# Sums of the modulation on VectorE in a two-layer transformer block, one core

## The chip, the cores and the metric

The kernel runs on one core of a Trainium2 chip. The metric is device time in microseconds (us) of one execution; each of the three runs shown is one such time. The engines are named as in the profile: PE is TensorE (PEld its weight loads), DVE is VectorE, ACT is ScalarE, POOL is GpSimd, SP is SyncE, which issues most of the DMAs.

## What is computed

Two layers work on 256 context rows and 256 latent rows of 1024 channels, in float32. Each layer first makes its modulation: six vectors of 1024 for each of two conditionings (latent and context), by a product of the conditioning's silu with a 1024 x 6144 matrix.

```python
# reference, cut: a layer's modulation feeds every norm and gate
# ada = silu(cond) @ w_ada[l] + b_ada[l]          # 6 x 1024 for c (latent rows) and c_ctx (context rows)
# h   = rmsnorm(x, g_pre_mix) * (1 + scale1) + shift1
# x  += gate1 * rmsnorm(token_mixer(h), g_post_mix)
# h   = rmsnorm(x, g_pre_ffn) * (1 + scale2) + shift2
# x  += gate2 * rmsnorm(swiglu(h), g_post_ffn)
def swiglu(h, wg, wu, wd):
    return (jax.nn.silu(h @ wg) * (h @ wu)) @ wd
```

The comment lines sum up how the norms, the gates and the modulation fit together; the token mixer has three parts side by side: an mLSTM, an hGRN2 and a differential attention, whose outputs are put together and multiplied by `w_out`. The second layer carries on the latent rows alone.

## The kernel before

A scheduler orders the instructions of each engine by priority and by what is ready; the order in which the Python code emits them is the first priority, and `high_priority` pulls some forward. Each engine then runs its list strictly in order.

**Weights.** Every large product splits its weights in two float32r parts. `wload` (L256) gets 512 KB by an SP DMA into `wraw` (three places), ACT casts it to `whi` (L272), DVE subtracts to get `wlo` (L273, two places each). PE then multiplies with `whi` and after that with `wlo` (L277). `gemm_tm`, `gemm_cm` and `gemm_bt` run this over parts of the contraction, and after each part call `ada_step` (L234), which advances the modulation by one step.

**Modulation.** `ada_group` (L186) works on one group of 1024-column pieces of `w_ada`; a group has two pieces (`ADA_COLS`, L184: what the norm before the mixers needs, both gates, what the norm before the feed-forward needs). For each of eight blocks of 128 channels it loads two pieces of 512 KB (`araw`, two places, and for the second layer some more places) and issues four matmuls (L204) of 128 x 512 columns, each against the 32 columns of `csil`, the silu of the conditionings. The four write to different quarters of one PSUM tile, `ada`; in the profile each appears as two records. Then DVE adds the bias (L209). Gates go over DRAM and come back as rows on all partitions (`gate_rows`, L431); the others are transposed (L224) to columns (`adaC`).

The first piece pair of layer 0 is made at the start in another way (`first_mod`) and isn't touched. `CFG` (L74) says where the other groups go: layer 0's gates beside its hGRN2, its feed-forward modulation beside its differential attention; layer 1's first group beside layer 0's feed-forward, its other two beside its own attention and mLSTM (`ada_rest`, L1008, and what is left after them).

**The stages on the time axis** (us of the profiled execution): start to 56; first hGRN2 projections and gates of the mLSTM 56 to 101; first two hGRN2 heads 101 to 129, the other two 165 to 195, projections between and after them to 235; differential attention 235 to 317; projections to 369; mLSTM 369 to 446, with its output products and the first norm; second norm and feed-forward 446 to 823; layer 1's first norm 823 to 862; its attention 1006 to 1071; its mLSTM and the norm after it 1107 to 1172; its feed-forward to the end.

Products of later projections fill PE in the stages that are chains of small steps (hGRN2, attention, mLSTM).

Of the kernel before, what the change touches and what calls it, by code (L numbers as in the profile page):

```python
# [102 lines left out]
def dit_block(ctx: ExitStack, tc: tile.TileContext, x, c, ctx_in, c_ctx, w_ada, b_ada, g_pre_mix,  # L103
# [81 lines left out]

    def ada_group(l, g):  # L186
        c01 = ADA_COLS[g]
        ba = par.tile([P, 512], F32, tag="ba", name=nm("ba"))
# [4 lines left out]
        ps = psa.tile([P, 512], F32, tag="ada", name=nm("ada"))
        for k in range(KD):
            if l == 1 and g > 0 and k % 3:
                # the places of the context's rows, which the last layer doesn't carry on
                p_, tag = ((yp, "Y"), (res, "R"))[k % 3 - 1]
                raws = [p_.tile([P, D], F32, tag=f"{tag}{i}", name=nm("araw")) for i in range(2)]
            else:
                raws = [wp.tile([P, D], F32, tag="araw", name=nm("araw"), bufs=2) for _ in range(2)]  # L200
            for i, c0 in enumerate(c01):
                SY.dma_start(out=raws[i], in_=w_ada[l, k * P:(k + 1) * P, c0:c0 + D])
# [7 lines left out]
        if g == 1:  # L210
            gp = par.tile([P, 512], F32, tag="gp", name=nm("gp"))
            G.memset(gp, 0.0)
            for r in range(2):
                for i, src in enumerate((g_post_mix, g_post_ffn)):
                    SY.dma_start(out=gp[64 * i + r:64 * i + r + 33:32, :], in_=src[l].rearrange("(j n) -> j n", j=2))
            G.tensor_tensor(gp, gp, ba, op=ALU.mult)
            gd = drp.tile([2, 2, D], F32, tag=f"gd{l}", name=nm("gd"))
            for j in range(4):
                G.dma_start(out=gd[j // 2, :, (j % 2) * 512:(j % 2 + 1) * 512], in_=gp[32 * j:32 * j + 2, :])
            ggd[l] = gd  # L220
# [1084 lines left out]
```

## Time and profile before

| | |
|---|---|
| median of 3 runs | 1374.21 us (1370.94 to 1379.26) |
| profiled execution, first to last instruction | 1371.2 us |
| PE busy (matmuls) | 1328.9 us, 97% |
| DVE busy | 754.6 us, 55% |
| ACT busy | 610.5 us, 45% |
| mean granted clock of PE | 0.995 of full |

The time of the profiled execution itself is shown only as that span; the median of the runs lies 3.0 us above it. Busy time is a share of the whole span and an average over stages; which wait ends last has to be read stage by stage.

### The profile page before, as it was taken

What the parts mean: (1) busy time and instruction counts of PE and PEld (TensorE: products, weight loads), DVE (VectorE), ACT (ScalarE), POOL (GpSimd) and SP (SyncE); (2) the same over time, 40 slices, a digit from 0 to 9 for tenths busy, and PEclk for the clock granted to TensorE, in tenths of its full rate; (3) what the DMA queues carried; (4) which work ended last, traced back from release to release, by engine and by line L of the source; (5) the groups of instructions that cost most, each with busy time, mean ns of one, the idle gap of its engine ahead of it and who ended that gap; (6) DMA issues with size and microseconds to landing.
All of it is one profiled execution on the core that took longest, in us unless ns stands there. A gap on an engine that the chain in (4) does not pass through costs nothing.

```text
span 1371.2 us, 25685 instructions
## 1 busy us (share of the span) xinstructions
PE 1328.9 (97%) x10422; PEld 1155.1 (84%) x10422; DVE 754.6 (55%) x1453; ACT 610.5 (45%) x1170; POOL 183.9 (13%) x310
## 2 busy tenths in 40 slices
PE   7999999999999999999999999999999998999997
PEld 5776889578899997998899888878966987899997
DVE  4657675455567752333332348487755455555555
ACT  3436352468455642222322246555435524544443
POOL 3201212121123100000000014133122101000001
PEclk9999999999999999999999999999999999999999
DMA  9752524532324674332333237723254434356563
GB/s 284 224 174 71 174 69 125 180 100 86 97 72 146 188 252 158 124 93 92 104 95 94 93 115 214 227 78 113 75 205 131 135 108 132 120 182 184 184 184 124
DMA packets 170772, 192.12 MB, mean 140 GB/s; under 512 B 10556, under 2 KB 158438, under 8 KB 170654
## 3 DMA queue, kind: packets, MB, share of 16 engines
q1 hardware_dynamic: 169230, 186.80, 43.7%
q0 software_dynamic: 1424, 3.68, 1.0%
q8 instruction: 82, 1.34, 0.4%
q14 instruction: 36, 0.29, 0.1%
HBM read 189.37 MB, written 1.08 MB: 139 GB/s over the span
## 4 chain that ended last, share of the span: by engine, by line
PE 81%; DVE 6%; ACT 5%; POOL 3%; DMA 2%; issue 2%; SPq 0%; DVEq 0%; POOLq 0%; ACTq 0%
PE mm L277 65%; PE ada L204 3%; PE mx L1084 2%; PE mx L929 2%; DVE wlo L273 1%; PE mm L1072 1%; ACT whi L272 1%; PE mx L951 1%; DMA araw<-in_w_ada_dram 1%; POOL rstd L379 1%; POOL Kh L783 1%; POOL rstd L378 1%; PE mx L407 1%; PE mx L827 1%; PE mx L945 1%
## 5 line engine op out<-in xcount | busy, mean ns | idle before, releaser
L272 ACT CAST whi<-wraw 128x1024 fp32r<-128x1024 f32 (+1 forms) x254 | 258.8, 1021 | 472.5 <-PE mm L277 436.3
L273 DVE TENSOR_TENSOR wlo<-wraw,whi 128x1024 fp32r<-128x1024 f32 (+1 forms) x250 | 299.8, 1201 | 286.7 <-PE mm L277 143.6
L277 PE MATMUL mm<-hT,whi 128*128 128x256 f32 (+1 forms) x1920 | 356.1, 336 | 0.6 <-ACT whi L272 0.6
L277 PEld LDWEIGHTS mm<-hT,whi 128*128 128x128 f32 x1920 | 293.8, 190 | 46.0 <-issue 5.8
L277 PE MATMUL mm<-whi,hT 128*128 128x256 f32 (+1 forms) x1792 | 262.6, 293 | 4.0 <-issue 1.5
L277 PEld LDWEIGHTS mm<-whi,hT 128*128 128x128 f32 x1792 | 231.8, 191 | 29.5 <-issue 17.9
L277 PE MATMUL mm<-hT,wlo 128*128 128x256 f32 (+1 forms) x960 | 185.2, 334 | 0.0
L277 PEld LDWEIGHTS mm<-hT,wlo 128*128 128x128 f32 x960 | 149.6, 190 | 17.4 <-issue 0.4
L277 PE MATMUL mm<-wlo,hT 128*128 128x256 f32 (+1 forms) x896 | 139.4, 293 | 0.1
L277 PE MATMUL mm<-whi,GT 128*128 128x256 f32 x1032 | 133.6, 284 | 0.3 <-ACT whi L272 0.3
L277 PEld LDWEIGHTS mm<-whi,GT 128*128 128x128 f32 x1032 | 128.0, 192 | 1.4 <-ACT whi L272 0.9
L277 PEld LDWEIGHTS mm<-wlo,hT 128*128 128x128 f32 x896 | 119.4, 192 | 10.8 <-issue 9.8
L1256 POOL TENSOR_TENSOR Z<-Z,gg 128x256 f32<-128x256 f32 x18 | 17.3, 975 | 457.5 <-ACT sqz L1255 457.4
L277 PE MATMUL mm<-wlo,GT 128*128 128x256 f32 x516 | 71.8, 284 | 0.3 <-DVE wlo L273 0.2
L277 PEld LDWEIGHTS mm<-wlo,GT 128*128 128x128 f32 x516 | 66.0, 192 | 1.5 <-DVE wlo L273 1.5
L204 PE MATMUL ada<-araw,csil 128*32 128x512 f32 x320 | 59.7, 603 | 0.7 <-DMA araw<-in_w_ada_dram 0.5
L1232 DVE TENSOR_TENSOR sg<-sg,mm 128x256 f32<-128x256 f32 (+1 forms) x48 | 25.0, 520 | 46.1 <-PE mm L277 45.2
L936 ACT ACTIVATE e<-mx,damx 128x512 f32<-128x512 f32 (+1 forms) x48 | 29.2, 616 | 37.2 <-DVE damx L933 37.1
L379 POOL TENSOR_TENSOR rstd<-rstd,mhalf 128x1 f32<-128x1 f32 (+2 forms) x58 | 39.7, 685 | 4.8
L378 POOL TENSOR_SCALAR rstd<-hss 128x1 f32<-128x1 f32 (+2 forms) x44 | 13.3, 303 | 200.2 <-ACT hsq L603 163.8
L758 ACT COPY Ck<-Kh 128x512 f32<-128x512 f32 (+1 forms) x56 | 28.7, 525 | 24.9 <-DVE Kh L783 17.2
L931 DVE TENSOR_REDUCE damx<-mx 128x1 f32<-128x512 f32 (+1 forms) x48 | 28.1, 598 | 20.2 <-PE mx L929 19.7
(267 smaller groups left out, 1386.2 us busy)
## 6 DMA issues: line engine op xcount, KB each, us to landing
araw<-in_w_ada_dram SPq DMA_DIRECT2D x80, 512.0 KB
wraw<-in_w_in_dram SPq DMA_DIRECT2D x68, 512.0 KB
wraw<-in_w_ffn_gate_dram SPq DMA_DIRECT2D x48, 512.0 KB
wraw<-in_w_ffn_up_dram SPq DMA_DIRECT2D x48, 512.0 KB
wraw<-in_w_ffn_down_dram SPq DMA_DIRECT2D x44, 512.0 KB
wraw<-in_w_out_dram SPq DMA_DIRECT2D x24, 512.0 KB
aw<-in_w_ada_dram SPq DMA_DIRECT2D x16, 512.0 KB
wraw<-in_w_in_dram SPq DMA_DIRECT2D x12, 256.0 KB
```

Of the source, the lines that this page charges most:

```text
L204: PE.matmul(ps[32 * j:32 * j + 32, :], lhsT=csil[:, k, :], rhs=raws[j // 2][:, (j % 2) * 512:(j % 2 + 1) * 512], start=k == 0, stop=k == K ...
L272: S.copy(hi[:, :nk, :n], raw[:, :nk, :n])
L273: (eng or V).tensor_tensor(lo[:, :nk, :n], raw[:, :nk, :n], hi[:, :nk, :n], op=ALU.subtract)
L277: PE.matmul(ps, lhsT=lhs, rhs=rhs, start=first, stop=last, skip_group_check=True)
L378: G.tensor_scalar(o[:, :width], ss, 1.0 / n, EPS, ALU.mult, ALU.add)
L379: G.tensor_tensor(o[:, :width], o[:, :width], mhalf[:, :width], op=ALU.pow)
L758: S.copy(C[:, q0:].rearrange("p (a b i) -> p b a i", b=2, i=m), vap(K_, 2 * m * pq0, [[512 + m, 2], [2 * m, np_], [1, m]]))
L929: PE.matmul(ps[:, :nk], lhsT=qkT[0][64 * j:64 * j + DA_D, h, t * P:(t + 1) * P], rhs=qkT[1][64 * j:64 * j + DA_D, h, :nk], start=True, sto ...
L931: V.reduce_max(mx[:, j:j + 1], ps[:, :nk], axis=AX.X)
L936: S.activation(e[:, j, :nk], pp[j][:, :nk], AF.Exp, bias=mx[:, 2 + j:3 + j], scale=sc, accum_out=mx[:, 4 + j:5 + j])
L1084: PE.matmul(po[:, i, d_, :], lhsT=W[d_, s_][0][:, t * P - W[d_, s_][2]:(t + 1) * P - W[d_, s_][2]], rhs=Vml[:, s_, h, :], start=n_ == 0, s ...
L1232: V.tensor_mul(sg[:, :n], sg[:, :n], ps)
```

## The change

`ada_group` no longer multiplies on PE for every block of channels. For each 512 KB block of `w_ada` DVE multiplies the rows with the conditioning's value for each channel (a scalar for each partition) and adds that to an accumulator of 128 x 1024, one for each conditioning: a `tensor_scalar_mul` for the first block, a `scalar_tensor_tensor` for each of the other seven. Only at the end of a group does PE multiply, with `esel`, a column of ones in the place of the conditioning, which adds up the 128 partitions: one matmul of 128 x 512 for each conditioning and each half piece.

The groups are now four (both gates apart), and where layer 1's context needs no modulation (all but its first group) only the latent conditioning is summed. The load of a block is issued one step ahead. Layer 0's first gate and its feed-forward modulation run from the first projections on, one step at each part of a product instead of at each second; their accumulators take the places of the residual rows R, which are loaded again before the first norm after the mixers. Layer 0's second gate and all four groups of layer 1 run from layer 0's output products on, beside its feed-forward. Nothing of the modulation is left beside the attention and the mLSTM of layer 1. The gate rows of the feed-forward are fetched at its last group of columns.

```diff
-CFG = (((2,), 2, 99), ((1, 2), 2, 3), 3)
...
-    ADA_COLS = ((0, D), (2 * D, 5 * D), (3 * D, 4 * D))
+    ADA_COLS = ((0, D), (2 * D,), (3 * D, 4 * D), (5 * D,))
-    def ada_group(l, g):
+    def ada_group(l, g, place):
         c01 = ADA_COLS[g]
+        kinds = (0, 1) if l < DEPTH - 1 or g == 0 else (0,)
+        ns = 2 * len(c01)
...
+        todo = [(i, k) for i in range(len(c01)) for k in range(KD)]
+        def load(i, k):
+            raw = wp.tile([P, D], F32, tag="araw", name=nm("araw"), bufs=2)
+            SY.dma_start(out=raw, in_=w_ada[l, k * P:(k + 1) * P, c01[i]:c01[i] + D])
+            return raw
+        raws = [load(*todo[0])]
+        accs = {}
+        for n_, (i, k) in enumerate(todo):
+            if n_ + 1 < len(todo):
+                raws.append(load(*todo[n_ + 1]))
+            raw = raws.pop(0)
+            if k == 0:
+                accs[i] = place(kinds)
+            for r in kinds:
+                a = accs[i][r]
+                if k == 0:
+                    V.tensor_scalar_mul(a, raw, csil[:, k, r:r + 1])
+                else:
+                    V.scalar_tensor_tensor(out=a, in0=raw, scalar=csil[:, k, r:r + 1], in1=a, op0=ALU.mult, op1=ALU.add)
+            yield
         ps = psa.tile([P, 512], F32, tag="ada", name=nm("ada"))
-        for k in range(KD):
...
-            for j in range(4):
-                PE.matmul(ps[32 * j:32 * j + 32, :], lhsT=csil[:, k, :],
-                          rhs=raws[j // 2][:, (j % 2) * 512:(j % 2 + 1) * 512],
-                          start=k == 0, stop=k == KD - 1, skip_group_check=True)
-            if k < KD - 1:
-                yield
-        V.tensor_add(ba, ps, ba)
+        for r in kinds:
+            for j in range(ns):
+                PE.matmul(ps[32 * j:32 * j + 32, :], lhsT=esel[:, r, :], rhs=accs[j // 2][r][:, (j % 2) * 512:(j % 2 + 1) * 512],
+                          start=r == 0, stop=r == kinds[-1], skip_group_check=True)
+        V.tensor_add(ba[:32 * ns], ps[:32 * ns], ba[:32 * ns])
...
-            pending += [ada_group(0, g) for g in (1, 2) if g not in CFG[0][0]]
-            pace[1] = 2
+            turn = [0]
+            def place0(kinds):
+                turn[0] ^= 2
+                return {r: res.tile([P, D], F32, tag=f"R{turn[0] + r}", name=nm("acc")) for r in kinds}
+            pending += [ada_group(0, g, place0) for g in (1, 2)]
...
-            lockstep(chain(da_tile(2), da_tile(0)), chain(da_tile(3), da_tile(1)), ada_rest, w_all)
+            lockstep(chain(da_tile(2), da_tile(0)), chain(da_tile(3), da_tile(1)), w_all)
         else:
-            lockstep(da_tile(2), da_tile(3), ada_rest, w_all)
+            lockstep(da_tile(2), da_tile(3), w_all)
...
         ada_flush()
+        if full:
+            load_rows()
...
         if l + 1 < DEPTH:
-            pending += [ada_group(1, g) for g in range(3) if g not in CFG[1][0]]
-            pace[1] = CFG[-1]
+            accq = stg.tile([P, 4, 768], F32, tag="qk", name=nm("accq"))
...
+            pending += [ada_group(l, 3, place1)] + [ada_group(l + 1, g, place1) for g in range(4)]
```

What it does to the order of the engines shows at three places. First DVE, in the first hGRN2 projections of layer 0, where `wlo` is made for the projections' products; before:

```order
L637 TENSOR_TENSOR Vhg_641<-mm_118,b_80_507 128x256
L656 TENSOR_SCALAR lf_897<-gt_632 128x32
L657 TENSOR_TENSOR lf_897<-lf_897,lft_898 128x32
L273 TENSOR_TENSOR wlo_749<-wraw_747,whi_748 128x1024
L273 TENSOR_TENSOR wlo_779<-wraw_777,whi_778 128x1024
```

and now (`acc` are the accumulators, L296 is the line of `wlo`):

```order
L665 TENSOR_TENSOR Vhg_645<-mm_118,b_84_511 128x256
L224 TENSOR_SCALAR acc_702<-araw_698,csil 128x1024
L224 TENSOR_SCALAR acc_703<-araw_698,csil 128x1024
L226 SCALAR_TENSOR_TENSOR acc_702<-araw_700,csil,acc_702 128x1024
L226 SCALAR_TENSOR_TENSOR acc_703<-araw_700,csil,acc_703 128x1024
L296 TENSOR_TENSOR wlo_708<-wraw_706,whi_707 128x1024
L296 TENSOR_TENSOR wlo_754<-wraw_752,whi_753 128x1024
L226 SCALAR_TENSOR_TENSOR acc_702<-araw_736,csil,acc_702 128x1024
```

Two to four products and sums of the modulation have come between one `wlo` and the next. Second DVE, in the mLSTM of layer 0, where `rd` (a reciprocal), `Oml` and `Y` are the small steps of one head; before:

```order
L1090 RECIPROCAL rd_4418<-rd_4418 128x4
L1090 RECIPROCAL rd_4451<-rd_4451 128x4
L1095 SCALAR_TENSOR_TENSOR Oml_4422<-mx_4403,rd_4418,Oml_4422 128x96
L1095 SCALAR_TENSOR_TENSOR Oml_4455<-mx_4436,rd_4451,Oml_4455 128x96
L1095 SCALAR_TENSOR_TENSOR Oml_4422<-mx_4403,rd_4418,Oml_4422 128x96
```

and now:

```order
L1108 RECIPROCAL rd_4410<-rd_4410 128x4
L226 SCALAR_TENSOR_TENSOR accq_5146<-araw_5473,csil,accq_5146 128x1024
L1113 SCALAR_TENSOR_TENSOR Oml_4414<-mx_4395,rd_4410,Oml_4414 128x96
L1108 RECIPROCAL rd_4443<-rd_4443 128x4
L1105 SCALAR_TENSOR_TENSOR rd_4476<-mx_4461,en_641 128x4
L226 SCALAR_TENSOR_TENSOR accq_5146<-araw_5473,csil,accq_5146 128x1024
L1113 SCALAR_TENSOR_TENSOR Oml_4414<-mx_4395,rd_4410,Oml_4414 128x96
```

Steps of 128 x 1024 stand between small steps of a head, and the `Oml` behind them waits for them in the queue. Third PE, at the start of layer 1's attention (`mx<-qkT,qkT` are its scores, `mm` the products that fill); before:

```order
L929 MATMUL mx_10696<-qkT_10621,qkT_10620 128x512
L204 MATMUL ada_10712<-araw_11119,csil 32x512 x2
L204 MATMUL ada_10712<-araw_11120,csil 32x512 x2
L929 MATMUL mx_10699<-qkT_10621,qkT_10620 128x512
L972 MATMUL mx_10721<-Mp_8756,ident_607 128x256
L204 MATMUL ada_11158<-araw_11159,csil 32x512 x2
L204 MATMUL ada_11158<-araw_11160,csil 32x512 x2
L277 MATMUL mm_11184<-whi_11186,hT_138 128x256
```

and now:

```order
L300 MATMUL mm_11267<-whi_11324,hT_142 128x256
L957 MATMUL mx_10884<-qkT_10820,qkT_10819 128x512
L957 MATMUL mx_10887<-qkT_10820,qkT_10819 128x512
L957 MATMUL mx_10895<-qkT_10820,qkT_10819 128x512
L300 MATMUL mm_11267<-whi_11324,hT_143 128x256
```

The modulation's matmuls are gone from there, and projection products stand in their place: between the first and the last score of layer 1's attention there are 164 matmuls of projections in the row of PE where there were 123, and no matmul of the modulation where there were 16.

## Rows read from the trace of the kernel before

**Rows 1.** The page: busy us, share of the span, instructions of each engine.

```profile
PE 1328.9 (97%) x10422; PEld 1155.1 (84%) x10422; DVE 754.6 (55%) x1453; ACT 610.5 (45%) x1170; POOL 183.9 (13%) x310
```

**Rows 2.** The page's chain that ended last: share by line.

```profile
PE mm L277 65%; PE ada L204 3%; PE mx L1084 2%; PE mx L929 2%; DVE wlo L273 1%; PE mm L1072 1%; ACT whi L272 1%; PE mx L951 1%; DMA araw<-in_w_ada_dram 1%; POOL rstd L379 1%; POOL Kh L783 1%; POOL rstd L378 1%; PE mx L407 1%; PE mx L827 1%; PE mx L945 1%
```

**Rows 3.** Who PE waited for: us in total, times, longest.

```profile
PE mx L165 <- DMA rowA<-in_b_ada_dram: 9.1, 1, 9.1
PE mx L407 <- DVE nsc L390: 8.9, 7, 4.7
PE mx L929 <- ACT e L936: 2.6, 4, 1.0
```

**Rows 4.** Stretches: length; busy of PE, PEld, DVE, ACT, POOL; clock; DMA share; GB/s.

```profile
56.00:101.40 45.40, 45.40 (x312) 34.21 (x311) 23.78 (x41) 17.86 (x26) 4.94 (x10) 1.00 0.53 169
101.40:128.90 27.50, 25.71 (x480) 17.67 (x471) 25.43 (x57) 20.23 (x42) 5.18 (x4) 1.00 0.31 98
128.90:235.00 106.10, 103.78 (x1202) 91.51 (x1200) 62.16 (x126) 42.91 (x77) 21.12 (x27) 0.98 0.35 107
235.00:317.00 82.00, 80.99 (x504) 55.18 (x502) 44.33 (x110) 46.27 (x120) 12.03 (x31) 1.00 0.45 147
369.00:446.00 77.00, 75.87 (x583) 70.72 (x584) 54.34 (x147) 42.36 (x113) 20.82 (x40) 1.00 0.33 105
446.00:823.00 377.00, 376.41 (x2336) 333.25 (x2336) 152.31 (x204) 123.61 (x173) 11.42 (x18) 1.00 0.41 128
1006.00:1071.00 65.00, 62.85 (x408) 42.84 (x407) 38.18 (x86) 35.14 (x96) 13.51 (x32) 1.00 0.49 167
```

**Rows 5.** Stretches, matmuls of L204 alone: length; busy of PE, PEld; clock; DMA; GB/s.

```profile
56.00:101.40 45.40, 3.20 (x24) 0.47 (x24) 1.00 0.53 169
101.40:128.90 27.50, 1.07 (x8) 0.16 (x8) 1.00 0.31 98
128.90:235.00 106.10, 5.30 (x32) 0.79 (x32) 0.98 0.35 107
235.00:317.00 82.00, 16.83 (x64) 2.30 (x64) 1.00 0.45 147
369.00:446.00 77.00, 3.15 (x10) 0.42 (x10) 1.00 0.33 105
446.00:823.00 377.00, 8.49 (x54) 1.23 (x54) 1.00 0.41 128
823.00:862.00 39.00, 4.03 (x24) 0.71 (x24) 1.00 0.72 205
1006.00:1071.00 65.00, 11.22 (x64) 1.85 (x64) 1.00 0.49 167
1107.00:1172.00 65.00, 6.37 (x40) 0.92 (x40) 0.96 0.36 114
sum 884.00, PE 59.65 PEld 8.86; mean PE 6.63 PEld 0.98
```

**Rows 6.** Timeline of PE in layer 0's attention: start, us, instruction, records merged.

```profile
252.55 1.04 PE L204 MATMUL ada<-araw,csil 128*32 128x512 f32 x2
253.53 0.66 PE L945 MATMUL mx<-ident,e 128*128 128x128 f32 x4
```

**Rows 7.** Instructions by line: duration in ns, min/median/max.

```profile
L427 DVE SCALAR_TENSOR_TENSOR R<-Z,rstd,R x14: 747/1279/1286, 434.8 to 1367.2; 128x1024 f32<-128x1024 f32 x10, 128x512 f32<-128x512 f32 x4
L390 DVE TENSOR_SCALAR nsc<-R,rstd x10: 752/754/756, 439.2 to 1168.4; 128x1024 f32<-128x1024 f32 x10
L379 POOL TENSOR_TENSOR rstd<-rstd,mhalf x58: 549/558/1752, 12.1 to 1167.8; 128x1 f32<-128x1 f32 x38, 128x2 f32<-128x2 f32 x16, 128x4 f32<-128x4 f32 x4
```

**Rows 8.** Groups by line on POOL: busy us, mean ns, idle before.

```profile
L379 POOL TENSOR_TENSOR rstd<-rstd,mhalf 128x1 f32<-128x1 f32 (+2 forms) x58 | 39.7, 685 | 4.8
```

**Rows 9.** What SP's queue waited for: us in total, times, longest.

```profile
SPq L269 <- DVE wlo L273: 761.0, 179, 21.5
```

More of the change, by code (lines that the diff above doesn't have):

```diff
@@ L149, in dit_block, with load_rows @@
             load_aw(aw0, 0, 1)
-    R = [res.tile([P, D], F32, tag=f"R{t}", name=f"R{t}") for t in range(4)]
-    for t in range(4):
-        SY.dma_start(out=R[t], in_=(ctx_in if t < 2 else x)[0, (t % 2) * P:(t % 2 + 1) * P, :])
+    R = [None] * 4
+    def load_rows():
+        for t in range(4):
+            R[t] = res.tile([P, D], F32, tag=f"R{t}", name=nm("R"))
+            SY.dma_start(out=R[t], in_=(ctx_in if t < 2 else x)[0, (t % 2) * P:(t % 2 + 1) * P, :])
+    load_rows()
     ident = const.tile([P, P], F32, tag="ident", name="ident")
@@ L175, in dit_block @@
             V.tensor_mul(csil[:, :, r], cc[:, 8 * r:8 * r + 8], sig[:, 8 * r:8 * r + 8])
+    esel = const.tile([P, 2, 32], F32, tag="esel", name="esel")
+    V.memset(esel, 0.0)
+    for r in range(2):
+        V.memset(esel[:, r, r:r + 1], 1.0)
     mhalf = const.tile([P, 16], F32, tag="mhalf", name="mhalf")
@@ L192, in ada_group @@
                 SY.dma_start(out=ba[64 * i + r:64 * i + r + 33:32, :], in_=b_ada[l, c0:c0 + D].rearrange("(j n) -> j n", j=2))
-        ps = psa.tile([P, 512], F32, tag="ada", name=nm("ada"))
-        for k in range(KD):
[L195 to L202, printed above, removed]
-            for j in range(4):
-                PE.matmul(ps[32 * j:32 * j + 32, :], lhsT=csil[:, k, :],
-                          rhs=raws[j // 2][:, (j % 2) * 512:(j % 2 + 1) * 512],
-                          start=k == 0, stop=k == KD - 1, skip_group_check=True)
-            if k < KD - 1:
-                yield
@@ L213, in ada_group @@
             for r in range(2):
[L214 to L220, printed above, removed]
+                SY.dma_start(out=gp[r:r + 33:32, :], in_=(g_post_mix, g_post_ffn)[g // 2][l].rearrange("(j n) -> j n", j=2))
@@ L221, in ada_group @@
+            G.tensor_tensor(gp, gp, ba[:64], op=ALU.mult)
+            gd = drp.tile([2, D], F32, tag=f"gd{l}{g}", name=nm("gd"))
+            for j in range(2):
+                G.dma_start(out=gd[:, j * 512:(j + 1) * 512], in_=gp[32 * j:32 * j + 2, :])
+            ggd[l, g // 2] = gd
         else:
@@ L432, in gate_rows @@
         t = p_.tile([P, D], F32, tag=f"gg{r}", name=nm("gg"))
-        G.dma_start(out=t, in_=ggd[l][which, r].partition_broadcast(P))
+        G.dma_start(out=t, in_=ggd[l, which][r].partition_broadcast(P))
         return t
@@ L999, in spaced @@
                     yield
-        grp = {g: ada_group(l, g) for g in CFG[l][0]}
-        def steps(g, n):
-            for i, _ in enumerate(g):
-                yield
-                if i == n - 1:
-                    return
-        ada_rest = spaced(chain(*[steps(grp[g], CFG[l][2] if g == 2 else 99) for g in CFG[l][0]]), CFG[l][1])
-        ada_flush()
         w_all = spaced(chain(*[ml_W(h, 1) for h in range(ML_H)]), WSP)
         if full:
-            lockstep(chain(da_tile(2), da_tile(0)), chain(da_tile(3), da_tile(1)), ada_rest, w_all)
+            lockstep(chain(da_tile(2), da_tile(0)), chain(da_tile(3), da_tile(1)), w_all)
         else:
-            lockstep(da_tile(2), da_tile(3), ada_rest, w_all)
+            lockstep(da_tile(2), da_tile(3), w_all)
         for i in range(3):
@@ L1181, in dit_block @@
             out_first(1)
-            for _ in ada_rest:
-                pass
             gg1 = {0: gate_rows(l, 0, 0, ggp)}
-        for _ in ada_rest:
-            pass
         dst_.close()
@@ L1191, in dit_block, with place1 @@
         if l + 1 < DEPTH:
-            pending += [ada_group(1, g) for g in range(3) if g not in CFG[1][0]]
-            pace[1] = CFG[-1]
+            accq = stg.tile([P, 4, 768], F32, tag="qk", name=nm("accq"))
+            turn1 = [0]
+            def place1(kinds):
+                turn1[0] ^= 1
+                if turn1[0]:
+                    return {r: vap(accq, D * r, [[1, D]]) for r in kinds}
+                return {r: ff.tile([P, D], F32, tag="acc", name=nm("acc")) if r else vap(accq, 2 * D, [[1, D]]) for r in kinds}
+            pending += [ada_group(l, 3, place1)] + [ada_group(l + 1, g, place1) for g in range(4)]
         with tc.tile_pool(name=f"ff{l}", bufs=1, reuse_waits="tile") as ff:
@@ L1196, in dit_block @@
             out_rest(halves[-1])
-            for _ in grp.get(2, ()):
-                pass
             u1, s1_ = mod_cols(l, 1)
@@ L1207, in dit_block @@
             Z = {t: yp.tile([P, D], F32, tag=f"Y{t}", name=nm("Z")) for t in qt}
-            gg = {r: gate_rows(l, 1, r, ggp) for r in ((0, 1) if full else (0,))}
             zss = {t: sm.tile([P, 4], F32, tag=f"zss{t}", name=nm("zss")) for t in qt}
@@ L1212, in dit_block @@
                 GT = {}
+                if gi == len(groups) - 1:
+                    gg = {r: gate_rows(l, 1, r, ggp) for r in ((0, 1) if full else (0,))}
                 alloc = lambda: [ff.tile([P, 2, 512], F32R, tag=f"GT{i}", name=nm("GT"), bufs=4) for i in range(2)]
```

5 lines of the change are left out of this document (3 added, 2 removed).

## The prediction

> **What bounds the kernel now.** I read the page's busy times first [rows 1]: PE is busy 97% of the span, DVE 55%, ACT 45%. Then the chain that ended last [rows 2]: 65% of it is the products (`mm`), the modulation's matmuls (L204) have 3%, DVE's `wlo` 1%. Third, whom PE waited for [rows 3]: a bias load at the start (9.1 us), the norm's `nsc` (8.9 us, 4.7 of it at one place), the attention's exponentials (2.6 us); after these come only smaller entries. So PE has work nearly always, and what is taken off PE is worth its time as long as the engine that takes it over does not make PE wait. DVE's 55% is an average, so the fourth view is the stretches [rows 4]: DVE is busy 25.43 of 27.50 us in the first two hGRN2 heads, 54.34 of 77 us in the mLSTM, 62.16 of 106.1 us from 129 to 235, but 152.31 of 377 us in the first feed-forward. Some stages have room for more on DVE and some have none.
>
> **What leaves PE.** 40 steps of four matmuls, 59.65 us of PE [rows 5]. The price differs by stage: 3.20, 1.07 and 5.30 us (24, 8 and 32 records) before 235 us, where a step costs about 1.2 us, but 16.83 us for 64 records in layer 0's attention and 11.22 us in layer 1's, over 1.4 us a step. So the dearest steps stand in the two attentions, where the change leaves few or none.
>
> **What comes to PE.** 32 ones-matmuls. A run of two records between its start and the next instruction takes 253.53 - 252.55 = 0.98 us [rows 6], and I take 1 us for each pass over up to four matmuls. There are 11 passes, and the order of PE splits up two of the groups, so about 13 us: 3 before 235 us, 2 in the attention of layer 0, 3 in its mLSTM, 5 in its feed-forward. Net, PE is rid of 59.65 - 13 = some 47 us; without anything else the time would be about 1328.
>
> **What comes to DVE.** 16 accumulators of eight blocks. The first block is a `tensor_scalar` of 128 x 1024 from float32 to float32; the nearest row is L390, 754 ns. The other seven are `scalar_tensor_tensor` of the same size; the nearest row is L427, 1279 ns at the median [rows 7]. One accumulator is 0.754 + 7 x 1.279 = 9.71 us, all 16 are 155 us. By the changed order of DVE they lie so: 56 to 101 us: 4 first blocks and 15 others, 22.2 us; 101 to 129: 2 others, 2.6; 129 to 235: 2 and 25, 33.5; layer 0's attention: none; its mLSTM: 3 and 14, 20.2; its feed-forward: 7 and 56, 76.9; layer 1: none. Added to DVE's busy time there [rows 4], that makes 46.0 of 45.4 us, 28.0 of 27.5, 95.7 of 106.1, 74.5 of 77 and 229 of 377 us. Two early stretches are over-full, the mLSTM is full, the feed-forward has room. That is where the sum is decided.
>
> **The sum, stage by stage.**
>
> 56 to 235 us: PE is rid of 9.57 and gets 3, so -7 if DVE hides everything. But from 56 to 129 us DVE has 74 us of work for 73 us, and in order: a `wlo` that stands behind four steps waits up to 4 x 1.28 = 5 us, and the product that wants it waits with it. If the 10 us by which DVE falls short (two stretches without a gap are never reached: I put its best share at nine tenths) come on top, and 5 of the 7 saved make up for it, the stage ends some us late; bounds -7 and +8. I take +1, nearer to the upper bound since DVE is already 92% busy in one of its stretches.
>
> 235 to 317 us, attention of layer 0: -16.83 + 2 = -14.8 of PE. The stage's PE is busy 80.99 of 82 us; DVE has 44.33 and ACT 46.27, so neither is near the end. The small steps of a head (scores, exponentials, normalizing) could become the limit as the filling gets less, so not all arrives: bounds -15 and -6, taken -12 (80%).
>
> 369 to 446 us, mLSTM: -3.15 + 2.9 = 0 on PE. On DVE 20.2 us come between the small steps of a head (`rd`, `Oml`, `Y`), each 1.28 us in front of an `Oml` that the output products wait for; with 74.5 of 77 us the stage has no slack. PE's cover is the products of the output. Bounds 0 and +9 (7 of the 14 longer steps on the path), taken +4.
>
> 446 to 823 us, feed-forward: -8.49 + 5 = -3.5 of PE. DVE gets 229 us of 377. `wlo` has two places, so it can be late by about one block of weights before PE stands; the load waits for `wlo` to free its place 179 times, 761 us together, at most 21.5 [rows 9], which shows that loads, `whi` and `wlo` run well ahead. Bounds -4 and +5 (four products late by 1.28 us), taken -2.
>
> 823 to 862 us, norm of layer 1: L204 has 4.03 us there, which partly fill PE's wait for the norm (the 4.7 us [rows 3]). Bounds -4 and 0, taken -2.
>
> 1006 to 1071 us, attention of layer 1: -11.22, nothing in return; PE 62.85 of 65, DVE 38.18, ACT 35.14 [rows 4]. Bounds -11 and -6, taken -9 (80%).
>
> 1107 to 1172 us, mLSTM of layer 1 and the norm: -6.37 [rows 5], but this stage is a chain over DVE's small steps and PE has a clock of 0.96 there, a sign of gaps. Bounds -6 and -1, taken -4.
>
> At nothing: the fetch of the gate rows (hidden by the group's remaining products), the second load of R (two transfers more in a queue whose engines are 0.33 busy in the mLSTM [rows 4]; without that cover some us in front of the norm) and the one-step-ahead loads of blocks.
>
> Sum: +1 - 12 + 4 - 2 - 2 - 9 - 4 = -24. The profiled span is 1371.2 us, so 1347; the median of the runs is 3.0 above that span, so **1350 us**. The bounds together are -47 and +9: 1327 to 1383.
>
> **Rivals.** *All of PE's time arrives.* For it: PE is 97% busy and `mm` has 65% of the chain [rows 1, 2]; against it, DVE's two over-full stretches. With nine tenths of the 47 us, 43, the time is 1374 - 43 = 1331; chance 0.2.
>
> *DVE becomes the bound in layer 0 (slower).* Before the bulk of the feed-forward 22.2 + 2.6 + 33.5 + 20.2 = 78.5 us of sums run, and some 7 more ahead of the first feed-forward products. DVE runs in order, so a `wlo` or a small step of hGRN2 or mLSTM waits behind them. It decides from the point at which about 43 us of them (34 of the 112 longer steps) lie on the path; at two thirds of 86, 57 us, the time is 1374 + 57 - 43 = 1388. Against it: before 235 us PE has other products to run while DVE is late, and 129 to 235 has 44 us of room. Chance 0.09.
>
> *The blocks stand in the way of the weights (same).* In the feed-forward up to two `araw` loads stand ahead of a `wraw` in SP's queue, and each waits until a DVE step has freed its place. If a weight is late by 1 us at 20 places, 20 of the 24 us are gone: 1370. For it: SP already waits for DVE's `wlo` most of its time [rows 9]; against it: these waits leave PE without one. Chance 0.1.
>
> *GpSimd and DVE hold each other up (same).* A small power on POOL (L379) takes 558 ns at the median and 1752 at most [rows 7]; its mean is 685 over 58 [rows 8], so such delays cost (685 - 558) x 58 = 7.4 us in all now. The new DVE steps read two tensors. If 16 powers in layer 0's mLSTM and norms each pay 1.2 us on the path, 19 of the 24 us are gone: 1369. Chance 0.05.
>
> A rule of the Trainium skill speaks for this last rival: the page "SBUF — State Buffer", section "SBUF: two separate sides", says that DVE with two SBUF inputs and a GpSimd instruction that reads SBUF share a port pair as an exclusive lock, so that one blocks while the other runs. By that rule, the spread of L379 (558 against 1752 ns [rows 7]) agrees with a wait behind about one such DVE step; that DVE caused it, no row shows.
>
> **Chances and range.** My forecast has 0.56, all of PE's time 0.2, the slower rival 0.09, the two others 0.15. About 0.5%, 6.9 us, is what a measurement of this kernel can tell from no change: faster means under 1367.3. Forecast and first rival are faster but for their upper edge, which makes 0.77; the two rivals near 1370, 0.14; slower 0.09. The range that should hold 8 in 10 leaves out the slower rival and the outer part of the first: 1330 to 1371.
>
> **What would show it.** Right: layer 0's attention shorter by about 12 us and layer 1's by 9; DVE's busy time near 755 + 155 = 910 us, the long steps at 1.28 us each; the first hGRN2 stretches no shorter, the mLSTM of layer 0 longer by some us; in the feed-forward no new waits of PE for `wlo` or weights. Wrong: PE waiting long for `wlo` between 56 and 129 us (DVE the bound, the slower rival); a feed-forward longer than before with waits for `wraw` (the third rival); powers on POOL mostly near 1.75 us; attention stages as long as before, which would mean that their heads' chains and not PE set their length; or long steps of well over 1.28 us, which raises every DVE term alike.

## The result: 14.8 us faster, where 24 were forecast

| | before | changed |
|---|---|---|
| median | 1375.34 us (1370.94 to 1379.26, 4 runs) | 1360.56 us (1359.11 to 1362.55, 4 runs) |
| ratio | | 0.9896, 95% interval 0.9874 to 0.9919 |
| profiled execution | span 1371.2 us | 1362.55 us, span 1360.8 us |
| PE idle within the span | 42.3 us | 66.3 us |

The page of the changed kernel, its busy times (busy us, share, instructions; before: [rows 1]), and the groups of the new lines (busy us and mean ns, then idle time before them):

```profile
PE 1294.5 (95%) x10166; PEld 1159.7 (85%) x10166; DVE 897.5 (66%) x1586; ACT 619.0 (45%) x1176; POOL 198.9 (15%) x316
...
L226 DVE SCALAR_TENSOR_TENSOR accq<-araw,csil,accq 128x1024 f32<-128x1024 f32 x63 | 81.3, 1295 | 25.9 <-DMA araw<-in_w_ada_dram 25.5
...
L226 DVE SCALAR_TENSOR_TENSOR acc<-araw,csil,acc 128x1024 f32<-128x1024 f32 x49 | 63.7, 1321 | 4.5 <-DMA araw<-in_w_ada_dram 4.4
```

Whom PE waited for now (us, times, longest; before: [rows 3]):

```profile
PE mx L430 <- DVE nsc L413: 13.2, 7, 7.9
PE mx L167 <- DMA rowA<-in_b_ada_dram: 9.6, 1, 9.6
PE mx L957 <- ACT e L964: 5.5, 6, 1.6
PE mx L795 <- ACT Ck L786: 5.1, 7, 2.4
PE mx L1128 <- DVE Y L638: 3.8, 2, 2.4
```

The longest wait, 7.9 us, is in layer 1's norm ahead of its feed-forward (`nsc` are the norm's scaled rows). PE's row there, first before, then changed (start, us, instruction, idle before it and what ended it):

```profile
1158.64 1.12 PE L277 MATMUL mm<-wlo,hT 128*128 128x256 f32 x8
1159.69 1.06 PE L204 MATMUL ada<-araw,csil 128*32 128x512 f32 x6
1162.40 0.66 PE L224 MATMUL mx<-ident,ba 128*128 128x128 f32 x4 [1.65 <-DVE ba L209]
1167.80 0.87 PE L407 MATMUL mx<-ident,nsc 128*128 128x128 f32 x3 [4.74 <-DVE nsc L390]
```

```profile
1147.93 1.12 PE L300 MATMUL mm<-wlo,hT 128*128 128x256 f32 x8
1156.92 0.87 PE L430 MATMUL mx<-ident,nsc 128*128 128x128 f32 x3 [7.87 <-DVE nsc L413]
```

From the end of the last product to the norm's first transposition 8.0 us passed before and 7.9 now. The old matmuls and transpositions there ran inside a wait whose length they did not set, so taking them away brought nothing at this place.

The prices were right: the sums last 145 us in their 112 longer steps (143 were reckoned), and the ones-matmuls 12.89 us of PE (13 were reckoned). DVE's busy time is 897.5 us and not 910: the records of neighbouring steps overlap by some 0.1 us (389.22 + 1.25 is behind 390.39 in DVE's row below). The 59.65 us of the old matmuls [rows 5] are gone from PE. But PE's other work became 12.4 us longer (1294.5 - 12.89 = 1281.6, against 1328.87 - 59.65 = 1269.2) and its idle time grew by 24.0. So -59.65 + 12.89 + 12.4 + 24.0 = -10.4, the difference of the spans. Of 47 us taken off PE, 36 were given back: two thirds as waits, one third as longer matmuls. The clock accounts for that third: the mean granted clock is 0.984, before 0.995, and by an estimate from these two, 1269.2 x (0.995 / 0.984 - 1) = 14 us.

Where: the time between two landmarks, which are instructions that both kernels have, from the timelines. `e` is the attention's exponentials, `mT` the start of the mLSTM, `sg` the feed-forward's gates, `ls` the gates of layer 1's first hGRN2. For example, the mLSTM's two landmarks of layer 0, first before, then changed:

```profile
367.90 0.58 ACT L1062 COPY mT<-mx 96x512 f32<-96x512 f32 x1 [1.31 <-PE mx L1058]
...
471.69 0.42 DVE L1232 TENSOR_TENSOR sg<-sg,mm 128x256 f32<-128x256 f32 x1 [1.48 <-PE mm L277]
```

```profile
354.12 0.58 ACT L1080 COPY mT<-mx 96x512 f32<-96x512 f32 x1 [1.31 <-PE mx L1076]
...
475.85 0.41 DVE L1254 TENSOR_TENSOR sg<-sg,mm 128x256 f32<-128x256 f32 x1
```

That is 103.8 us before and 121.7 now, 18 more. All stages, as differences from before in us; e1 to e8 are the experiments below. The forecast's borders are other ones, up to some 50 us away, and products of later stages move over a border with the order of PE, so a row of this table holds its term of the forecast only roughly:

| stage | forecast | changed | e1 | e4 | e5 | e8 |
|---|---|---|---|---|---|---|
| start to first `e`, layer 0 | +1 | -3.6 | -4.4 | -3.2 | -2.0 | -3.5 |
| attention 0, to `mT` | -12 | -10.2 | -10.3 | -7.5 | -9.3 | -9.2 |
| mLSTM 0, to first `sg` | +4 | +18.0 | +0.3 | +5.2 | +1.5 | +2.0 |
| feed-forward 0, to last `sg` | -2 | -5.3 | +18.4 | -2.8 | -6.1 | -2.9 |
| to `ls`, layer 1 (down products, norm) | -2 | +4.2 | +2.2 | +3.2 | -0.4 | +3.0 |
| to first `e`, layer 1 | 0 | -1.2 | -1.3 | -1.3 | -0.8 | -1.3 |
| attention 1, to `mT` | -9 | -9.3 | -7.7 | -9.3 | -4.4 | -7.8 |
| mLSTM 1 and norm, to first `sg` | -4 | -2.8 | -2.5 | -2.6 | -2.4 | -3.6 |
| sum | -24 | -10.2 | -5.3 | -18.3 | -23.9 | -23.3 |

The mLSTM of layer 0 missed its term by 14 us. The forecast let it end at 446 us; nearer to that lies the first `nsc` of the norm behind it (at 439.2 us in both kernels). The stretches up to it and from it to the first `sg`, first before, then changed (length; busy of PE, PEld, DVE, ACT, POOL; clock; DMA share; GB/s):

```profile
367.90:439.20 71.30, 71.23 (x557) 67.34 (x556) 49.35 (x139) 38.91 (x107) 19.31 (x37) 1.00 0.30 97
439.20:471.69 32.49, 30.82 (x240) 28.09 (x239) 24.57 (x35) 22.68 (x38) 6.48 (x12) 1.00 0.60 188
```

```profile
354.12:439.20 85.08, 78.67 (x575) 72.33 (x573) 69.74 (x159) 41.04 (x109) 24.49 (x36) 0.96 0.40 126
439.20:475.85 36.65, 32.52 (x242) 31.18 (x242) 33.50 (x46) 23.08 (x41) 10.15 (x18) 0.91 0.61 190
```

So up to the forecast's border it is +13.8, and +4.2 behind it. DVE's row shows why:

```profile
389.13 0.17 DVE L1108 RECIPROCAL rd<-rd 128x4 f32<-128x4 f32 x1
389.22 1.25 DVE L226 SCALAR_TENSOR_TENSOR accq<-araw,csil,accq 128x1024 f32<-128x1024 f32 x1
390.39 0.30 DVE L1113 SCALAR_TENSOR_TENSOR Oml<-mx,rd,Oml 128x96 f32<-128x96 f32 x1
390.62 1.33 DVE L226 SCALAR_TENSOR_TENSOR accq<-araw,csil,accq 128x1024 f32<-128x1024 f32 x1
...
393.09 0.30 DVE L1113 SCALAR_TENSOR_TENSOR Oml<-mx,rd,Oml 128x96 f32<-128x96 f32 x1
393.32 1.32 DVE L226 SCALAR_TENSOR_TENSOR accq<-araw,csil,accq 128x1024 f32<-128x1024 f32 x1
394.57 1.30 DVE L296 TENSOR_TENSOR wlo<-wraw,whi 128x1024 fp32r<-128x1024 f32 x1
396.73 0.55 DVE L638 SCALAR_TENSOR_TENSOR Y<-Oml,rstd,Y 128x96 f32<-128x96 f32 x2 [0.86 <-POOL rstd L402]
```

Steps of 0.17 and 0.30 us, each of which releases the next step of a head, stand behind sums of 1.3 us; PE then waits for `Y`, 2.4 us at one place. The stage in four stretches, changed:

```profile
354.00:392.00 38.00, 37.15 (x284) 34.85 (x283) 29.93 (x75) 17.84 (x53) 11.99 (x19) 1.00 0.28 87
392.00:406.00 14.00, 10.23 (x56) 9.49 (x55) 12.39 (x24) 6.28 (x13) 4.53 (x6) 0.76 0.55 181
406.00:440.00 34.00, 31.91 (x242) 28.39 (x240) 28.32 (x62) 17.73 (x47) 8.19 (x13) 1.00 0.48 151
440.00:476.00 36.00, 32.17 (x240) 31.04 (x241) 32.87 (x44) 22.43 (x39) 9.94 (x18) 0.91 0.60 187
```

PE stands for 10.5 us of these 122 (1.7 of the 104 before), and in the two stretches with the most waits the granted clock has a mean of 0.76 and 0.91; these are means over its two levels, 1.00 and 0.50 (2.4 and 1.2 GHz).

### The profile page after: what moved, and what is told of

Same layout as the page of the kernel before. It is cut to its first block, busy times and chain, and to the rows that moved or that the text cites. A ratio compares the mean times of both kernels' runs of the same rounds, so it can differ in the third digit from the quotient of the medians.

```text
span 1360.8 us, 25400 instructions
## 1 busy us (share of the span) xinstructions
PE 1294.5 (95%) x10166; PEld 1159.7 (85%) x10166; DVE 897.5 (66%) x1586; ACT 619.0 (45%) x1176; POOL 198.9 (15%) x316
## 4 chain that ended last, share of the span: by engine, by line
PE 79%; DVE 8%; ACT 5%; POOL 3%; issue 2%; DMA 2%; SPq 0%; DVEq 0%; POOLq 0%; ACTq 0%
PE mm L300 65%; PE mx L1102 2%; DVE wlo L296 2%; PE mx L957 1%; PE mx L979 1%; ACT whi L295 1%; PE mm L1090 1%; POOL rstd L402 1%; PE mx L430 1%; PE mx L973 1%; ACT Dt L1011 1%; DMA wraw<-in_w_ffn_down_dram 1%; PE mx L855 1%; PE ada L231 1%; POOL rstd L401 1%
## 5 line engine op out<-in xcount | busy, mean ns | idle before, releaser
L296 DVE TENSOR_TENSOR wlo<-wraw,whi 128x1024 fp32r<-128x1024 f32 (+1 forms) x250 | 299.5, 1199 | 199.5 <-ACT whi L295 97.0
L300 PEld LDWEIGHTS mm<-hT,whi 128*128 128x128 f32 x1920 | 296.9, 192 | 42.5 <-issue 3.3
L300 PE MATMUL mm<-whi,hT 128*128 128x256 f32 (+1 forms) x1792 | 265.7, 294 | 4.5 <-ACT hT L1133 2.2
L300 PEld LDWEIGHTS mm<-whi,hT 128*128 128x128 f32 x1792 | 234.5, 193 | 22.3 <-issue 10.5
L226 DVE SCALAR_TENSOR_TENSOR accq<-araw,csil,accq 128x1024 f32<-128x1024 f32 x63 | 81.3, 1295 | 25.9 <-DMA araw<-in_w_ada_dram 25.5
L300 PE MATMUL mm<-wlo,GT 128*128 128x256 f32 x516 | 71.3, 283 | 0.7 <-DVE wlo L296 0.7
L226 DVE SCALAR_TENSOR_TENSOR acc<-araw,csil,acc 128x1024 f32<-128x1024 f32 x49 | 63.7, 1321 | 4.5 <-DMA araw<-in_w_ada_dram 4.4
L401 POOL TENSOR_SCALAR rstd<-hss 128x1 f32<-128x1 f32 (+2 forms) x44 | 17.0, 386 | 242.7 <-ACT hsq L631 159.0
L957 PE MATMUL mx<-qkT,qkT 48*128 48x512 f32 (+1 forms) x96 | 34.2, 562 | 6.3 <-ACT e L964 5.5
```

Of the source, the lines that this page charges most:

```text
L226: V.scalar_tensor_tensor(out=a, in0=raw, scalar=csil[:, k, r:r + 1], in1=a, op0=ALU.mult, op1=ALU.add)
L296: (eng or V).tensor_tensor(lo[:, :nk, :n], raw[:, :nk, :n], hi[:, :nk, :n], op=ALU.subtract)
L300: PE.matmul(ps, lhsT=lhs, rhs=rhs, start=first, stop=last, skip_group_check=True)
L401: G.tensor_scalar(o[:, :width], ss, 1.0 / n, EPS, ALU.mult, ALU.add)
L957: PE.matmul(ps[:, :nk], lhsT=qkT[0][64 * j:64 * j + DA_D, h, t * P:(t + 1) * P], rhs=qkT[1][64 * j:64 * j + DA_D, h, :nk], start=True, sto ...
```

## Experiments

Theory A: DVE's sums, in its in-order row, make PE wait. Theory B: the old matmuls had filled PE's waits in chains of small steps, so that part of what they cost was never on the path. Theories C to E stand in the expectations.

**e1: no sums in the mLSTM.** The late accumulators take a place that comes free with the second norm:

```diff
-            accq = stg.tile([P, 4, 768], F32, tag="qk", name=nm("accq"))
...
                 norm_T(u1, s1_, hf, scr)
+            if l + 1 < DEPTH:
+                accq = ff.tile([P, 4, 768], F32, tag="nsc", name=nm("accq"))
+                pending += [ada_group(l, 3, place1)] + [ada_group(l + 1, g, place1) for g in range(4)]
```

> The changed kernel with one move: the accumulators of layer 0's second gate and of layer 1's four groups take a place that only comes free with layer 0's second norm, so that none of their sums can stand in DVE's row between the small steps of layer 0's mLSTM (17 stood there); they all run in the first feed-forward. Theory A (the sums in DVE's in-order row between small steps made PE wait 6.3 us from 360 to 439 us, and the waits then cost clock): that stage gets back 6 to 10 us and the feed-forward hides the 20 us of sums, so 1351 to 1355 against 1360.6. Theory B (the small steps' own chain sets the stage once the modulation's matmuls are gone as filling): the waits stay, 1359 to 1362. Theory C (the feed-forward is then over-full, DVE some 216 of 346 us, and lets wlo come late): 1363 to 1368, with PE waits for wlo there.

1369.81 us (1367.17 to 1373.04), ratio 0.9968 (0.9954 to 0.9982): slower than the changed kernel, and above the ranges of all three theories. Yet the mLSTM got back what theory A said and more, 17.7 us. Not all of that is the sums': with them go 2.95 us of ones-matmuls, and 20 products (511 run there, 531 in the changed kernel) come after the first `sg` again, some 3.4 us at e8's 331 us for 1972 records (below). By this estimate some 11 us are the sums'. And though nothing of the modulation is left in this stage, it is as long as before, when 4.19 us of old matmuls stood in it. Taking those away gained nothing there, as theory B says.

What the mLSTM got back was lost again in the feed-forward, 18.4 us longer than before. Theory C named that place and was 2 us off the total; but its cause, `wlo` late, isn't what PE waited for there (457 to 825 us):

```profile
PE mm L300 <- ACT GT L1257: 6.0, 1, 6.0
PE mm L300 <- DVE sg L1256: 3.0, 1, 3.0
PE mm L300 <- ACT sg L1251: 2.2, 2, 1.8
```

It is again small steps behind sums, `sg` and `GT` (the gated products) this time. Ahead of the 6.0 us, DVE's and then ACT's row:

```profile
555.82 2.48 DVE L226 SCALAR_TENSOR_TENSOR accq<-araw,csil,accq 128x1024 f32<-128x1024 f32 x2 [0.88 <-DMA araw<-in_w_ada_dram]
558.22 1.28 DVE L1256 TENSOR_TENSOR sg<-sg,mm 128x512 f32<-128x512 f32 x2
```

```profile
558.93 1.22 ACT L1257 CAST GT<-sg 128x512 fp32r<-128x512 f32 x2 [6.73 <-DVE sg L1256]
```

**e2, e3, e4: what the sums cost.** The longer steps add 8 of 1024 columns, in the early groups (e2, shown), in the late ones (e3), in all (e4):

```diff
+                    n8 = 8 if l == 0 and g < 3 else D
-                    V.scalar_tensor_tensor(out=a, in0=raw, ..., in1=a, ...)
+                    V.scalar_tensor_tensor(out=a[:, :n8], in0=raw[:, :n8], ..., in1=a[:, :n8], ...)
```

> Leaves out work: the sums of layer 0's first gate and of its feed-forward modulation add 8 of the 1024 columns only (42 steps, so some 53 us less on DVE before 235 us; all loads, waits and matmuls stay). Theory A (sums in DVE's row are what eats the freed PE time): the hGRN2 stages lose their new waits, some 3 to 6 us, 1355 to 1358. Theory B (chains of small steps): within 2 us of 1360.6. Before the chip I forecast a cost of 8 us at most for this place.

> Leaves out work: the sums of layer 0's second gate and of layer 1's groups add 8 of the 1024 columns only (70 steps, some 90 us less on DVE in layer 0's mLSTM and its feed-forward; all loads, waits and matmuls stay). Theory A: as in e1_late or a little more, 1348 to 1354, nearly all of it from 360 to 476 us. Theory B: 1359 to 1362. If the feed-forward's sums cost by themselves, this is faster than e1_late by that cost.

> Leaves out work: all 112 longer sums add 8 columns only. What is left is PE's saving without DVE's price. Theory A: the saving arrives but for the norm between the layers, 1340 to 1347, and PE waits little more than the 42 us of the kernel before. Theory B: 1356 to 1361, PE's waits stay at some 66 us.

e2: 1361.78 us (1360.14 to 1362.6), no gain. e3: 1353.05 (1349.15 to 1354.43). e4: 1352.38 (1351.34 to 1354.15). So the early sums cost nothing that shows, although DVE was busy 44.53 of 45.4 us from 56 to 101 us in the changed kernel; the late ones cost some 8 us; and with nearly no sums at all only 22 of the 47 us arrive (ratio 0.9847). Theory A's range held for e3 and theory B's for e2; both missed e4, A too low and B too high. So A explains the smaller part of what was given back. e4's account: 46.6 off PE, idle +18.3, other matmuls +9.5 us.

e3 keeps 7.1 us of the mLSTM's 18, e1 0.3. Of that difference 3.14 us are the ones-matmuls, which e3 leaves in this stage and e1 doesn't. The short steps also still stand in DVE's row and wait there for their `araw`, 7.0 us in four waits. In the changed kernel DVE has no such wait from 353 to 476 us, so this belongs to e3's short steps; what it costs was not measured by itself.

**e5: the kernel before, its matmuls cut.** Seven of eight blocks multiply 8 of 512 columns:

```diff
+                n8 = 512 if k == 0 else 8
-                          rhs=raws[j // 2][:, (j % 2) * 512:(j % 2 + 1) * 512],
+                          rhs=raws[j // 2][:, (j % 2) * 512:(j % 2) * 512 + n8],
```

> The kernel before, and leaves out work: of each group of eight blocks, seven multiply 8 of 512 columns (all loads, waits and instructions stay), which takes some 50 us off PE and adds nothing to any engine. Theory B (the chains of small steps end the stages once the modulation's matmuls are gone as filling, and PE's waits cost clock besides): 20 to 30 us arrive, as in e4_short_all (22), so 1345 to 1355, with PE idle some 15 to 20 us more than before (42 us) and a granted clock lower than 0.995. Rival D (the removal itself arrives in full and e4_short_all loses to the new order of the planner and to waits for loads on DVE): 1325 to 1333.

1347.98 us (1341.92 to 1351.65), ratio 0.98 (0.9766 to 0.9835). These matmuls now last 17.92 us, so 41.7 us left PE, and 27 arrived (24 by the spans), with no new step in DVE's row (the scheduler did order part of it anew). Idle time grew by 8.4 us, where 15 to 20 were expected, and the other matmuls by 9.4; 2.5 of the 8.4 us are waits of the short matmuls for their own loads. This is theory B without any sum in the way. The wait in layer 1's norm is the same 7.9 us as in the changed kernel. Rival D, by which all of it arrives, falls.

**e6: filling put back.** 16 matmuls of no use in layer 1's late norm, so many passes of four ahead of each pair of channel blocks:

```diff
+    def filler(x):
+        ps = psa.tile([P, 512], F32, tag="ada", name=nm("fill"))
+        for j in range(4):
+            PE.matmul(ps[32 * j:32 * j + 32, :], lhsT=esel[:, 0, :], rhs=x[:, (j % 2) * 512:(j % 2 + 1) * 512], ...)
...
-    late_norm = lambda ...: norm_T(u, s, 1, scr, xs)
+    late_norm = lambda ...: norm_T(u, s, 1, scr, xs, (1, 0, 1, 2))
```

> The changed kernel with 16 matmuls of no use (four passes of four, 32 columns by 512, on rows that the norm has just made) in layer 1's late norm, where the kernel before had 22 records of the modulation and a granted clock of 1.00, and the changed kernel waits 3.8 us and runs at 0.91 from 822 to 880 us. Theory B: PE's clock stays at its higher level there and the products behind the norm run as in the kernel before, 3 to 4 us less, 1357. Rival E (the norm's own chain over DVE and ACT ends that stage whatever PE does, or the useless matmuls stand in the way of the transposes): 1360 to 1363.

The norm in three kernels (stretches as above; PE, PEld, DVE, ACT, POOL, then the clock): before, changed, e6.

```profile
850.00:857.00 7.00, 5.24 (x29) 4.25 (x28) 5.56 (x10) 3.94 (x7) 3.02 (x6) 1.00 0.80 198
857.00:864.00 7.00, 7.00 (x49) 4.29 (x48) 5.93 (x12) 5.13 (x9) 0.00 (x0) 1.00 0.63 189
```

```profile
850.00:857.00 7.00, 4.67 (x22) 3.53 (x22) 5.37 (x8) 3.81 (x6) 3.15 (x7) 0.97 0.82 181
857.00:864.00 7.00, 4.88 (x21) 4.38 (x20) 5.49 (x12) 4.27 (x8) 0.00 (x0) 0.50 0.50 136
864.00:871.00 7.00, 7.00 (x34) 6.97 (x33) 3.71 (x5) 3.47 (x5) 0.00 (x0) 0.80 0.27 76
```

```profile
857.00:864.00 7.00, 7.00 (x51) 4.61 (x44) 6.21 (x12) 5.06 (x9) 0.00 (x0) 1.00 0.51 135
864.00:871.00 7.00, 7.00 (x39) 6.69 (x38) 4.86 (x8) 2.96 (x3) 0.00 (x0) 1.00 0.64 170
```

Without the modulation's matmuls PE stood 2.1 us of these 7 and ran at half clock (1.2 instead of 2.4 GHz); with useless ones in their place it stays at 1.00, and from the norm's last `nsc` to `ls` the time is 20.6 us, in the changed kernel 23.2, before 20.3. But how long PE runs at the lower level there differs between executions of one kernel. e8 and e9 (below) are the same kernel; the stretch in each:

```profile
844.40:866.00 21.60, 19.00 (x93) 17.20 (x94) 13.82 (x29) 13.26 (x19) 0.00 (x1) 0.92 0.54 147
```

```profile
844.20:867.40 23.20, 21.03 (x93) 19.33 (x94) 13.80 (x29) 13.39 (x19) 0.00 (x0) 0.78 0.51 141
```

So the filling is worth 1.0 to 2.6 us in this stage, by the clock. The total, 1361.1 us (1357.39 to 1361.96), doesn't show it: it lies in rival E's range and not at theory B's 1357. By the trace 1.3 us went again behind the last `sg`, and 1.2 and 1.5 us in the two attentions, where the mean clock was 0.98 and in the changed kernel's trace 1.00.

**e7 and e8: places by what was learnt.** e7: layer 0's second gate summed in the attention, layer 1's groups only after four half blocks of the feed-forward, the two-sum group last. e8: the same without sums in the attention:

```diff
-                pending += [ada_group(l, 3, place1)] + [ada_group(l + 1, g, place1) for g in range(4)]
...
+                    if gi == 0 and bi == 4 and l + 1 < DEPTH:
+                        pending += [ada_group(l, 3, place1)] + [ada_group(l + 1, g, place1) for g in (1, 2, 3, 0)]
```

> Places chosen by the runs so far: as e1_late, but layer 0's second gate is summed in layer 0's attention (behind the other two groups, in the places of R), and layer 1's groups start only after the first four half blocks of the feed-forward, those for the latent rows alone first, so that never more than two to four sums stand between two wlo. If the mLSTM's loss comes from sums in its row and e1_late's loss of 18 us in the feed-forward from sums that stand dense ahead of sg and GT: the mLSTM as in e1_late (15 us ahead of the kernel before), the feed-forward no longer than in the kernel before, the attention some 3 us slower for its 16 sums: 1345 to 1350. If the feed-forward loses whenever it has all of layer 1's sums: 1360 to 1365.

> As e7_mix2, but layer 0's second gate stays in the feed-forward, first in the row, and the attention has no sums. If sums in the attention cost (they stand between its scores' steps): 2 to 4 us faster than e7_mix2, 1343 to 1348. If 20 us more of sums in the feed-forward cost more than in the attention: slower than e7_mix2, 1350 to 1358.

e7: 1356.29 us (1355.91 to 1358.18), slower than expected: the attention kept 2 us less than e8 and the feed-forward was 4.8 us longer, though DVE has 16 steps of the modulation fewer in it. PE waits there for `GT`, 2.2 and 1.4 us, amid the two-sum group, which starts at 668 us and in e8 at 718; that this is the cause was not tested. **e8: 1350.02 us** (1347.91 to 1350.65), ratio 0.9817 (0.9794 to 0.984), 6.3 us under e7, where 2 to 4 were expected, and as fast as e4 that leaves the sums out. The feed-forwards of e1 and e8, from first to last `sg`:

```profile
457.00:809.00 352.00, 339.63 (x1988) 296.33 (x1987) 218.04 (x246) 94.87 (x120) 12.85 (x17) 0.99 0.57 179
```

```profile
461.00:792.00 331.00, 331.00 (x1972) 290.94 (x1970) 214.78 (x243) 94.75 (x120) 12.69 (x17) 1.00 0.60 191
```

DVE is busy 218 and 215 us, PE stands 12.4 us in one and not at all in the other. How much DVE does can't be what decides here; what differs is what stands in front of what.

**e9 to e12: which part of e8 does it, and the filling once more.**

> The kernel of e8_late2 once more, beside the next one and for its ratio: 1348 to 1352.

> e8_late2 with the 16 useless matmuls of e6_fill in layer 1's late norm. Theory B: the clock stays at its higher level there and the stage is 2 to 3 us shorter, as in the trace of e6_fill; if the later stages keep that, 1346 to 1349, 2 to 3 us under e9_late2_again. Rival E (what the norm gives back is lost again in a later stage, as the end of e6_fill's trace hints): equal within 1 us.

> e1_late with the start after four half blocks of the feed-forward alone; the groups stay in their order, so that layer 1's first group (two sums for each block) comes second. If e1_late lost by sums ahead of the first sg and GT steps: most of its 18 us come back, 1351 to 1355. If it lost by the two-sum group amid the first blocks, dense sums whenever they come: 1358 to 1366.

> e1_late with the order of the groups alone (those of one sum for each block first, the two-sum group last), the start at the feed-forward's first product. If the first sg and GT steps are what matters: little comes back, 1362 to 1368. If it is the density amid the first blocks: 1351 to 1356.

| | groups in their order | two-sum group last |
|---|---|---|
| start at the first product | e1: 1369.81 | e12: 1372.58 (0.9975) |
| start after four half blocks | e11: 1359.15 (0.9878) | e8, e9: 1350.02, 1349.05 (0.9806) |

The start matters most, the order helps only with it. e12 is slower than both of its ranges; e11 lies in its second range, but not for the reason given there. In e11 the feed-forward to its last `sg` is only 2.2 us longer than in e8, but the last group's sums are late (eight steps of the modulation start after the last `sg`, none in e8) and run on into the down products, where PE waits 3.2 us for `whi` at one place and 2.7 for the norm at another; e11 loses 7 to 9 of its 10 us there. e10 has 1348.16 us (1346.24 to 1349.64), 0.9 under e9, as rival E said: its norm has 20.6 us, 2.6 less than e9 and 1.0 less than e8, but against this spread the total's gain is neither shown nor excluded.

## Why the prediction held, and where its size was off

Direction and range held (1350, 1330 to 1371; measured 1360.56), and PE was the bound. That the miss stayed at 11 us is partly luck: two terms were too pessimistic (by 4.6 and 3.3 us) and made up for part of the two that were too optimistic (by 14 and 6). By its terms:

- **mLSTM of layer 0, the step that failed**: +4 with bounds 0 and +9, measured +18, and +13.8 up to the first `nsc`. The argument was right (long steps ahead of `Oml`, none of the stage's time free), but the term counted 14 long steps once, at 1.28 us and at most half of them on the path. It left out that the products behind take up the delay with new waits up to the norm (PE stands 10.5 us, before 1.7), that PE's clock falls where it waits (0.76 from 392 to 406 us), and that taking the old matmuls away gains nothing there (e1), so that the -3.15 could not make up for the new 2.9. By e1 some 11 us are the sums', as waits and clock together.
- **Norm between the layers**: -2, measured +4.2. The 4.7 us of [rows 3] were put here, but stand at 1167.8 us, in layer 1's norm ahead of its feed-forward. That L204's 4.03 us fill waits here was right, but their loss was put at nothing; e6 and e10 price it at 1.0 to 2.6 us, by the clock.
- **mLSTM 1 and its norm**: -4, measured -2.8. Of 6.37 us off PE less than half arrived: the misplaced wait is here, 4.7 us before and 7.9 now.
- **56 to 235 us**: +1, measured -3.6 up to the first `e`. Too pessimistic on DVE, whose over-full row cost nothing that shows (e2). Even so only 3.6 of the 10.6 us that left PE there arrived, in e4 with nearly no sums 3.2: sums can't be what ate the rest, and the old matmuls' cover, as in e5 (2.0 there), is the likely cause.
- **The attentions**: -12 and -9, measured -10.2 and -9.3. That four fifths arrive was too low. Of the first attention's 16.83 us 4.0 stand ahead of its first `e`; between the landmarks 12.83 us left and 1.92 came, so 10.2 of 10.9 arrived. In layer 1 38 products moved ahead of the first `e`, so it and the stage ahead of it have to be read together: 10.5 of 11.2 us. e4's 7.5 and e5's 4.4 are the clock for the most part: it has a mean of 0.97 and 0.96 there, which is some 3 us of each, and 1.00 in the changed kernel's attentions.
- **Feed-forward**: -2, measured -5.3; 20 products that now run ahead of the first `sg`, some 3.4 us, are in that.
- **At nothing**: the second load of R shows no cost. e1 and e8 keep it, and have 71.7 us from `mT` to the first `nsc` (before 71.3).
- **Rivals.** That all of PE's time arrives falls with e5: 27 of 41.7 us did, with no new work anywhere. That DVE becomes the bound in layer 0 happened in part, at one stage and not by its load. Blocks ahead of the weights: the first feed-forward is 5.3 us shorter, so not there. GpSimd and DVE holding each other up falls as a cost: the power on POOL has 561 ns at the median and 676 in the mean (558 and 685 before [rows 7, 8]) with 112 more DVE steps of two inputs. The chance of 0.77 for faster is a slip; forecast and first rival have 0.76 together.

```profile
L402 POOL TENSOR_TENSOR rstd<-rstd,mhalf x58: 547/561/1933, 12.3 to 1156.9; 128x1 f32<-128x1 f32 x38, 128x2 f32<-128x2 f32 x16, 128x4 f32<-128x4 f32 x4
```

The two longest powers of the changed kernel, 1933 and 1912 ns, each start while a DVE step with two inputs from SBUF runs, and go on after it has ended; the longest one, beside two of the new sums:

```profile
151.18 2.47 DVE L226 SCALAR_TENSOR_TENSOR acc<-araw,csil,acc 128x1024 f32<-128x1024 f32 x2
152.59 1.93 POOL L402 TENSOR_TENSOR rstd<-rstd,mhalf 128x4 f32<-128x4 f32 x1
```

The Trainium skill's page "SBUF — State Buffer", section "SBUF: two separate sides", says that DVE with two inputs from SBUF and a GpSimd step that reads SBUF block each other. These rows agree with that, but no run here shows a loss of time from it.

Where e8's remaining 18.0 us of new idle time stand can be read from the stretches between the landmarks (us of PE standing):

| stage | before | changed | e5 | e8 |
|---|---|---|---|---|
| start to first `e`, layer 0 | 16.0 | 20.2 | 19.6 | 21.3 |
| attention 0 | 1.3 | 4.8 | 2.8 | 4.7 |
| mLSTM 0 | 1.7 | 10.5 | 3.1 | 4.2 |
| feed-forward 0 | 0.0 | 0.0 | 0.0 | 0.0 |
| to `ls`, layer 1 | 3.4 | 8.0 | 3.8 | 7.3 |
| to first `e`, layer 1 | 3.4 | 3.5 | 3.7 | 3.4 |
| attention 1 | 2.1 | 2.5 | 1.6 | 2.5 |
| mLSTM 1 and norm | 6.9 | 9.5 | 8.8 | 9.6 |
| the rest | 7.5 | 7.3 | 7.4 | 7.3 |

What stays open is how much of it filling could win back: only the late norm was tried by itself. In the first of these stages the first hGRN2 pair ends 3 to 7 us later than before in e1, e4, e5 and e8, and the second pair at most 0.5 us later.
